# w_down's long passes: four pairs a half in seven products, in the order of gate and up, and loads queued as buffers come free

## The chip, the cores and the metric

The kernel runs on one core of one Trainium2 chip. The metric is the device time of one launch in microseconds (us). Before the change it is 1049.4 us, the median of three runs (1048.66 to 1050.55).

## The reference, cut to what matters

One transformer layer over 256 tokens of width 2048, all in fp32. The first part (input projection, attention, convolution, output projection) is left as it is by the change. The second part is a SwiGLU feed-forward with hidden width 5632:

```python
hn = rms_norm(h, norm2_g)
a  = einsum('bsd,df->bsf', hn, w_gate)          # 2048 x 5632
bu = einsum('bsd,df->bsf', hn, w_up)            # 2048 x 5632
h  = h + einsum('bsf,fd->bsd', silu(a) * bu, w_down)   # 5632 x 2048
```

## The kernel before

**Splitting.** TensorE multiplies in a rounded format, so every fp32 operand is split into a rounded part `hi` and a residue `lo = x - hi`, and a product takes three matmuls: hi·hi, lo·hi, hi·lo. Weights come in by DMA on SP's queue. ScalarE (ACT) rounds them to `whi` (L320). VectorE (DVE) makes the residue `wlo` (L329). For some weights a DMA on GpSimd's (POOL's) queue makes it instead: ACT writes the negated rounding (L323) and the DMA accumulates the raw weight onto it (L324).

**Units.** Gate, up and down work in *units* on 128x512 weight tiles. A *two* is two row tiles of one weight (`g` the first column block, `u` the second), 12 matmuls, one load of 512 KB, one `whi`, one `wlo`. A *pair* (`s`) takes two row tiles of both column blocks at once and multiplies them by a Strassen scheme in seven products instead of eight: 21 matmuls for what two twos do in 24. It costs more beside TensorE: two loads of 512 KB into `wb`, three sums on DVE (`wt`, L966 to L968), two roundings on ACT (`wh`, L969 and L972), two residues on DVE (`wlb` L975, `wlt` L976). All seven products of a pair write PSUM banks `q`, and when the last pair of a block is done `bank_sums` (L1092 to L1099) combines the banks on ACT and DVE.

**Blocks and groups.** The hidden width is worked in 11 blocks of 512, in groups of 4, 4 and 3. After the blocks of a group, `down_pass` multiplies their activations by the rows of w_down that belong to them, in two *halves* of 1024 output columns each. A gate/up block (from the second on) has four pairs and eight twos in the order `sggsggsuusuu`. A half of a long down pass (a group of four blocks) has two pairs and twelve twos, `gguuggsguugsuu` and `sgggugggusuuuu`. The results are added to `hd` in DRAM by accumulating DMAs on POOL's queue (L1138, L1155).

**Activations.** At the end of a block, `block_done` adds the last banks (L1113), multiplies gate by up (L1115), and `transposed` turns the product on TensorE (`ps_a`, L831) and splits it into `ahi` and `alo` (L840, L842). The operands of the down pairs are seven sums of activations, split as well; `make_down_forms` makes them during the last blocks of a group.

**Order.** Each engine runs its instructions in the order in which the program issues them. `run_chunks` issues unit after unit: loads and roundings up to three units ahead, residues two units ahead. Generators (`start`, `resume`, `lag`) put the work between blocks a given number of half units later. DVE and ACT are therefore queues: a late instruction holds up all that stand behind it.

Of the kernel before, what the change touches and what calls it, by code (L numbers as in the profile page):

```python
# [12 lines left out]
F32 = mybir.dt.float32  # L13
# [5 lines left out]
P = 128  # L19
# [76 lines left out]

HI_AHEAD, LO_AHEAD = 3, 2

PAIR_AHEAD = 6

FIRSTS = [sum(FGROUPS[: g + 1]) for g in range(len(FGROUPS))]

# [20 lines left out]
def tile_block(  # L123
# [262 lines left out]

    def run_chunks():
        n = len(chunks)
        i = j = p = 0
        behind = [k for k in range(n) if chunks[k].get("kind") == "s"][NS]  # L390
        for t in range(n):
            hi_lead, lo_lead = lead(t)
            while j < min(i, t + 1 + lo_lead):
                chunks[j]["split"](chunks[j])
                j += 1
            while p < min(n, t + 1 + PAIR_AHEAD):
                if chunks[p].get("kind") == "s":

                    if p < behind and p > t + hi_lead:
                        break  # L400
                    load_pair(chunks[p])
                p += 1
            while i < min(n, t + 1 + hi_lead):
                if i in before:
                    before[i]()
                chunks[i]["load"](chunks[i])
                chunks[i]["round"](chunks[i])
                i += 1
                if hi_lead == lo_lead:
                    chunks[j]["split"](chunks[j])  # L410
                    j += 1
            while j < min(n, t + 1 + lo_lead):
                chunks[j]["split"](chunks[j])
                j += 1
            chunks[t]["multiply"](chunks[t])
# [403 lines left out]
        yield from transposed(j, aa)  # L819

    def transposed(j, aa):
        last = j + 1 in FIRSTS
        b = j - group_of(j)[1]
        for t in range(N // P // 2):

            pool_, tag = (acc_ps, "acc") if last else (aux_ps, "aux")
            pt = pool_.tile([P, 2, S], F32, tag=tag, name="ps_a")
            for i in range(2):
                for m in range(NM):
                    c = (2 * t + i) * P  # L830
                    pe.transpose(pt[:, i, m * P : (m + 1) * P], aa[m][:, c : c + P], ident)  # L831
            if b < 2 and 2 * t < ND:
                raw_act[b] = lhs.tile([P, 2, S], F32, tag=("lhi", "llo")[b], name=f"ar{j}")
                act.copy(raw_act[b], pt)
                yield from lag(3 if last else 6)
                if b:
                    start(make_down_forms(group_of(j)[0]))
# [19 lines left out]

    def make_down_forms(g):

        fp = ffn["pool"]  # L860
        gap = lambda: lag(5 if FGROUPS[g] == 4 else 2)
        a11, a21 = (raw_act[0][:, :, m * P : (m + 1) * P] for m in range(NM))
        a12, a22 = (raw_act[1][:, :, m * P : (m + 1) * P] for m in range(NM))

        hi = fp.tile([P, 7, ND, P], F32R, tag="dhi", name="dhi")
        lo = fp.tile([P, 3, ND, P], F32R, tag="dlo", name="dlo")
        fa, fb = (lhs.tile([P, 2, ND, P], F32, tag=t, name="dsums") for t in ("lhi", "llo"))
        act.copy(hi[:, 0], a11)
        dve.scalar_tensor_tensor(fa[:, 0], a21, -1.0, a22, ALU.mult, ALU.subtract)
        yield from gap()  # L870
        act.copy(hi[:, 1], a12)
        dve.scalar_tensor_tensor(fa[:, 1], fa[:, 0], -1.0, a11, ALU.mult, ALU.subtract)
        yield from gap()
        act.activation(hi[:, 2], a22, AF.Copy, scale=-1.0)
        dve.tensor_tensor(fb[:, 0], a11, a21, ALU.subtract)
        yield from gap()
        act.copy(hi[:, 3:5], fa)
        dve.tensor_tensor(fb[:, 1], a12, fa[:, 1], ALU.subtract)
        yield from gap()
        act.copy(hi[:, 5:7], fb)  # L880
        for i, a in ((0, a11), (1, a12)):
            dve.tensor_tensor(lo[:, i], a, hi[:, i].bitcast(F32), ALU.subtract)
            yield from gap()
        dve.scalar_tensor_tensor(lo[:, 2], a22, -1.0, hi[:, 2].bitcast(F32), ALU.mult, ALU.subtract)
        yield from gap()
        pairs = [lhs.tile([P, 2, ND, P], F32R, tag=t, name="dlo2") for t in ("lhi", "llo")]
        for i, f in ((0, fa), (1, fb)):
            dve.tensor_tensor(pairs[i], f, hi[:, 3 + 2 * i : 5 + 2 * i].bitcast(F32), ALU.subtract)
            yield from gap()
        los = [lo[:, 0], lo[:, 1], lo[:, 2], pairs[0][:, 0], pairs[0][:, 1], pairs[1][:, 0], pairs[1][:, 1]]  # L890
        down_forms[g] = {f: (hi[:, i], los[i]) for i, f in enumerate((0, 1, 3, 4, 5, 6, 2))}

    forms = {}
# [144 lines left out]
    def fast_block(order, pairs, twos, sources, operands, half, whole, by_dma=dict(g=(), u=())):  # L1040

        units, sums = [], {}
        left = dict(s=list(pairs), g=list(twos), u=list(twos))
        for kind in order:
            what = left[kind].pop(0)
            c = dict(kind=kind, sums=sums, done=None, first={}, last={}, rows=what["rows"], **operands)
            if kind == "s":
                c.update(p=what["p"], load=lambda c: None, round=round_pair, split=split_pair, multiply=multiply_pair,
                         uses=[q for q, _, _ in PRODUCTS])
# [12 lines left out]
        units[-1].update(done=whole, prompt=True)  # L1062
        chunks.extend(units)
# [8 lines left out]

    def down_pass(g, j0, nb):
        k0 = j0 * HD
        ks = [k for k in range(nb * HD) if k >= 2 * HD or k % HD >= ND]
        twos = [dict(ks=(k0 + a, k0 + b), rows=slice(k0 + a, k0 + b + 1, b - a), k=None)
                for a, b in zip(ks[::2], ks[1::2])]
        for i, order in enumerate(DORDERS[nb]):
            n = 2 * i
            end = {}  # L1080
            fast_block(order, [dict(p=p, rows=slice(k0 + p, k0 + p + HD + 1, HD)) for p in range(ND)], twos,
                       dict(g=(w_down, n * N), u=(w_down, (n + 1) * N)),
                       dict(pairs=lambda: down_forms.get(g), plain=actT.get),
                       lambda sums, n=n, end=end: down_half(g, n, sums, end),
                       lambda sums, n=n, end=end: down_whole(g, n, sums, end))

    halfway = {}

# [19 lines left out]
    def block_done(j, q):  # L1108
# [4 lines left out]
            dve.tensor_tensor(u[m], q[i], u[m], ALU.add)  # L1113
# [18 lines left out]

    def down_half(g, n, q, end):
        gs, us = yield from bank_sums(q)
        for m in range(NM):
            cs = slice(n * N, (n + 1) * N)
            if not at_end(g, n):
# [10 lines left out]
    def down_whole(g, n, q, end):  # L1148
# [3 lines left out]
        for m, i in enumerate((Q3, QX)):  # L1152
            if not at_end(g, n):
                dve.tensor_tensor(us[m], q[i], us[m], ALU.add)
                pool.dma_start(out=hd[m][:, (n + 1) * N : (n + 2) * N], in_=us[m], accum_op=ALU.add)  # L1155
                continue
            w = N // 2
            for a in range(0, N, w):
                hs = hend[m][:, N + a : N + a + w]
                dve.tensor_tensor(hs, hs, q[i][:, a : a + w], ALU.add)  # L1160
                sp.dma_start(out=out[m * P : (m + 1) * P, (n + 1) * N + a : (n + 1) * N + a + w], in_=hs)
        if g == len(FGROUPS) - 1 and not at_end(g, n):
            fetch_end()

# [82 lines left out]
```

## Time and profile before

| | |
|---|---|
| median of 3 runs | 1049.4 us |
| profiled execution | 1048.92 us, span 1047.1 us |
| PE busy | 1036.2 us, 99% |
| DVE busy | 900.6 us, 86% |
| ACT busy | 621.6 us, 59% |
| granted TensorE clock | 1.00 |

The page gives busy time for each engine, and the chain of waits that ended last. A matmul's row shows how long it is in flight, about 390 ns, and matmuls overlap: what one costs is the distance from its start to the next one's. The timeline view lists instructions of an engine in order of time with start and duration; in square brackets stands idle time before it and what ended that.

### The profile page before, as it was taken

The numbers are of one execution on the slowest core, as the hardware profiler recorded it, in microseconds if no ns is written. First come the engines' busy times: TensorE is split into PE (matmuls) and PEld (weight loads), VectorE is DVE, ScalarE is ACT, GpSimd is POOL, SyncE is SP. The second block draws the span as 40 slices with busy tenths as digits, with TensorE's granted clock in tenths as the row PEclk, the third lists the DMA queues.
The fourth block names the chain that finished last, engine by engine and source line by source line (L and its number), as shares of the span: only waits on it lengthen the run. The fifth ranks groups of instructions, "written<-read, shape, count | busy, mean of one in ns | idle before, by whom it ended". The sixth has DMA issues, their size and how long they took to land.

```text
span 1047.1 us, 12933 instructions
## 1 busy us (share of the span) xinstructions
PE 1036.2 (99%) x4663; PEld 852.5 (81%) x4663; DVE 900.6 (86%) x1095; ACT 621.6 (59%) x786; POOL 100.5 (10%) x143
## 2 busy tenths in 40 slices
PE   9999999999999999999999999999999999999998
PEld 7888887877788788888888888888888888888886
DVE  7899889898765599999787898999878789989897
ACT  7544666755756565776463657666644446657442
POOL 0130122201100100000001010000000110000010
PEclk9999999999999999999999999999999999999999
DMA  9657654453546566987867789879757879798683
GB/s 335 227 182 280 212 163 167 154 181 134 177 153 226 194 223 214 268 266 236 232 210 188 217 271 273 256 217 285 248 175 241 219 208 291 222 287 267 187 265 85
DMA packets 113936, 231.30 MB, mean 221 GB/s; under 512 B 7504, under 2 KB 8656, under 8 KB 113616
## 3 DMA queue, kind: packets, MB, share of 16 engines
q1 hardware_dynamic: 104864, 203.71, 56.9%
q0 software_dynamic: 8864, 26.74, 13.4%
q8 instruction: 36, 0.59, 0.2%
q14 instruction: 28, 0.23, 0.1%
q10 hardware_dynamic: 144, 0.03, 0.0%
HBM read 204.24 MB, written 9.44 MB: 204 GB/s over the span
## 4 chain that ended last, share of the span: by engine, by line
PE 61%; DMA 2%; DVE 2%; issue 1%; ACT 0%; DVEq 0%; POOLq 0%
PE q L1020 12%; PE q L1014 12%; PE q L1015 12%; PE q L995 8%; PE q L993 7%; PE q L994 7%; DMA raw<-in_w_down_dram 1%; PE ps_a L831 1%; DMA wlo<-raw 1%; PE acc L365 1%; PE acc L359 1%; PE acc L360 1%; DVE wlo L329 1%; DVE wlt L976 0%; DVE wt L966 0%
## 5 line engine op out<-in xcount | busy, mean ns | idle before, releaser
L320 ACT CAST whi<-raw 128x1024 fp32r<-128x1024 f32 (+1 forms) x273 | 281.5, 1048 | 141.6 <-PE acc L360 58.9
L329 DVE TENSOR_TENSOR wlo<-raw,whi 128x1024 fp32r<-128x1024 f32 (+1 forms) x239 | 287.8, 1218 | 73.5 <-ACT whi L320 73.3
L972 ACT CAST wh<-wt 128x2048 fp32r<-128x2048 f32 x52 | 99.6, 1914 | 77.6 <-DVE wt L968 76.9
L976 DVE TENSOR_TENSOR wlt<-wt,wh 128x2048 fp32r<-128x2048 f32 x52 | 119.1, 2290 | 14.9 <-ACT wh L972 14.7
L359 PE MATMUL acc<-whi,xhi 128*128 128x512 f32 x320 | 126.9, 397 | 1.0 <-ACT whi L320 0.9
L360 PE MATMUL acc<-whi,xlo 128*128 128x512 f32 x320 | 125.2, 391 | 0.0
L1014 PE MATMUL q<-whi,chi 128*128 128x512 f32 x320 | 125.2, 391 | 0.0
L1015 PE MATMUL q<-whi,clo 128*128 128x512 f32 x320 | 124.5, 389 | 0.0
L993 PE MATMUL q<-wh,fhi 128*128 128x512 f32 x280 | 109.9, 393 | 0.0
L994 PE MATMUL q<-wh,flo 128*128 128x512 f32 x280 | 109.1, 390 | 0.0
L517 DVE SCALAR_TENSOR_TENSOR y<-upad,cw,y 128x256 f32<-128x256 f32 x240 | 102.2, 482 | 2.2 <-ACT y L510 2.2
L1014 PE MATMUL q<-whi,ahi 128*128 128x512 f32 x256 | 100.2, 391 | 0.0
L1015 PE MATMUL q<-whi,alo 128*128 128x512 f32 x256 | 99.6, 389 | 0.0
L975 DVE TENSOR_TENSOR wlb<-wb,wh 128x1536 fp32r<-128x1536 f32 x52 | 91.1, 1752 | 1.8 <-ACT wh L969 1.8
L365 PE MATMUL acc<-wlo,xhi 128*128 128x512 f32 x320 | 87.8, 396 | 2.0 <-DVE wlo L329 2.0
L1020 PE MATMUL q<-wlo,chi 128*128 128x512 f32 x320 | 85.7, 390 | 0.2 <-DMA wlo<-raw 0.2
L969 ACT CAST wh<-wb 128x1536 fp32r<-128x1536 f32 x52 | 76.6, 1474 | 0.0
L365 PEld LDWEIGHTS acc<-wlo,xhi 128*128 128x128 f32 x320 | 59.7, 189 | 15.3 <-DVE wlo L329 3.3
L359 PEld LDWEIGHTS acc<-whi,xhi 128*128 128x128 f32 x320 | 60.4, 189 | 14.3 <-ACT whi L320 1.9
L1020 PEld LDWEIGHTS q<-wlo,chi 128*128 128x128 f32 x320 | 59.9, 188 | 13.2 <-DMA wlo<-raw 0.8
L360 PEld LDWEIGHTS acc<-whi,xlo 128*128 128x128 f32 x320 | 60.4, 189 | 12.2
L1014 PEld LDWEIGHTS q<-whi,chi 128*128 128x128 f32 x320 | 60.1, 188 | 12.3
(230 smaller groups left out, 1739.1 us busy)
## 6 DMA issues: line engine op xcount, KB each, us to landing
raw<-in_w_in_dram SPq DMA_DIRECT2D x79, 512.0 KB, 4.6
raw<-in_w_down_dram SPq DMA_DIRECT2D x64, 512.0 KB, 7.2
raw<-in_w_gate_dram SPq DMA_DIRECT2D x48, 512.0 KB, 7.5
raw<-in_w_up_dram SPq DMA_DIRECT2D x48, 512.0 KB, 6.2
wb<-in_w_up_dram SPq DMA_DIRECT2D x40, 512.0 KB, 3.7
wb<-in_w_gate_dram SPq DMA_DIRECT2D x40, 512.0 KB, 4.9
wlo<-raw POOLq DMA_DIRECT2D x34, 512.0 KB, 7.1
raw<-in_w_out_dram SPq DMA_DIRECT2D x32, 512.0 KB, 4.2
```

The costliest lines, as they stand in the source:

```text
L320: act.copy(c["hi"], c["raw"])
L329: dve.tensor_tensor(c["lo"], c["raw"], c["hi"].bitcast(F32), ALU.subtract)
L359: pe.matmul(ps[m], xhi[:, ms], hi[:, j, :], start=c["first"] and j == 0, stop=False)
L360: pe.matmul(ps[m], xlo[:, ms], hi[:, j, :], start=False, stop=False)
L365: pe.matmul(ps[m], xhi[:, ms], lo[:, j, :], start=False, stop=c["last"] and j == nk - 1)
L517: dve.scalar_tensor_tensor(y[:, ct, :], src, wk, y[:, ct, :], ALU.mult, ALU.add)
L976: dve.tensor_tensor(lot, c["t"], c["hi"][:, :SUMMED].bitcast(F32), ALU.subtract)
L993: pe.matmul(ps, hi, c["hi"][:, w], start=bool(first), stop=False)
L994: pe.matmul(ps, lo, c["hi"][:, w], start=False, stop=False)
L1014: pe.matmul(ps, xs[i][0][:, ms], hi[:, i, :], start=i == 0 and bool(c["first"].get(qs[m])), stop=False)
L1015: pe.matmul(ps, xs[i][1][:, ms], hi[:, i, :], start=False, stop=False)
L1020: pe.matmul(sum_bank(c, qs[m]), xs[i][0][:, ms], lo[:, i, :], start=False, stop=i == 1 and bool(c["last"].get(qs[m])))
```

## The change

It does four things.

- The long passes (`NDS = (4, 4, 2)`, two before) take four pairs and eight twos a half, in the order of gate and up, `sggsggsuusuu`. The short pass keeps its orders.
- The residues of three twos a half (the third `g`, the second and fourth `u`) come by DMA on POOL's queue; before, a down pass had none.
- The forms of the down pairs grow with it: operands of 128x512 instead of 128x256, eleven instructions on DVE. All activations of a group's first two blocks are kept raw.
- Weight loads of all later blocks are issued in the order in which their buffers come free (`load_freed`). Lags around the ends of blocks and the accumulating DMAs move (`HD_LAG`, `closing`).

```diff
-ND = 2
-DORDERS = {4: ("gguuggsguugsuu", "sgggugggusuuuu"), 3: ("gguusggsuu", "gggsgsuuuu")}
+NDS = (4, 4, 2)
+DORDERS = {4: (ORDER, ORDER), 3: ("gguusggsuu", "gggsgsuuuu")}
+HD_LAG = 3
+DOWN_BY_DMA = {4: (dict(g=(2,), u=(1, 3)),) * 2, 3: (dict(g=(), u=()),) * 2}
...
+        def freed(side, t):
+            if not ahead[side]:
+                return None
+            k = (raws, pairs)[side][place[side][ahead[side][0]] - (RAW_BUFS, PAIR_BUFS)[side]]
+            return k if k in split and (t >= k or not chunks[k]["by_dma"]) else None
+
+        def load_freed(t):
+            while True:
+                ready = [(k, side) for side in range(2) if (k := freed(side, t)) is not None]
+                if not ready:
+                    return
+                load(ahead[min(ready)[1]].pop(0))
...
-            yield from lag(1 if last else 4)
+            yield from lag(1 if last else 3 if closing(j) else 4)
+
+    def closing(j):
+        return j + 1 in FIRSTS and NDS[group_of(j)[0]] == HD
...
+        one = lambda tag, dt, name: lhs.tile([P, 4, P], dt, tag=tag, name=name)[:, :nd]
...
+        f4, f5, f6, f2 = (one(t, F32, "dsums") for t in ("lhi", "lhi", "llo", "llo"))
...
+        dve.tensor_tensor(lo[3], f2, hi[3].bitcast(F32), ALU.subtract)
+        yield from gap()
+        ls = ffn["pool"].tile([P, 4, nd, P], F32R, tag="draw", name="dls")
+        act.copy(ls[:, 3], f6)
+        for i, (f, h) in enumerate(((f4, hs[:, 0]), (f5, hs[:, 1]), (f6, ls[:, 3]))):
+            dve.tensor_tensor(ls[:, i], f, h.bitcast(F32), ALU.subtract)
...
-        yield from lag(4)
+        yield from lag(6 if closing(j) else 4)
         yield from transposed(j, u)
...
+        if not at_end(g, n):
+            if FGROUPS[g] > 3:
+                yield from lag(HD_LAG)
+            for m in range(NM):
+                pool.dma_start(out=hd[m][:, (n + 1) * N : (n + 2) * N], in_=us[m], accum_op=ALU.add)
```

On DVE, where the last gate/up block of a long group ends and its down pass begins (before: `sum` is what `bank_sums` and `block_done` write, `wlo` the residue of a two, `wt` a sum of a pair):

```order
L1094 TENSOR_TENSOR sum_4695<-q_4424,sum_4694 128x512
L1095 TENSOR_TENSOR sum_4696<-q_4428,sum_4695 128x512
L1096 TENSOR_TENSOR sum_4697<-q_4432,sum_4696 128x512
L1097 TENSOR_TENSOR sum_4695<-q_4432,sum_4695 128x512
L1098 TENSOR_TENSOR sum_4694<-q_4444,sum_4694 128x512
L1099 TENSOR_TENSOR sum_4696<-q_4436,sum_4696 128x512
L329 TENSOR_TENSOR wlo<-raw,whi 128x1024
L1113 TENSOR_TENSOR sum_4695<-q_4449,sum_4695 128x512
L1113 TENSOR_TENSOR sum_4697<-q_4627,sum_4697 128x512
L1115 TENSOR_TENSOR sum_4695<-sum_4695,sum_4694 128x512
L1115 TENSOR_TENSOR sum_4697<-sum_4697,sum_4696 128x512
L329 TENSOR_TENSOR wlo<-raw,whi 128x1024 x3
```

The same place after the change, from the last residue before it on (`dls` are residues of the down pairs' forms, on line 933; the sums are now L1140 to L1145, L1159 and L1161, the pair's sums L1011 to L1013, its residues L1020 and L1021):

```order
L331 TENSOR_TENSOR wlo<-raw,whi 128x1024
L933 TENSOR_TENSOR dls<-dsums,dhs 128x512 x2
L1011 TENSOR_TENSOR wt<-wb 128x1024
L1012 TENSOR_TENSOR wt<-wb,wt 128x512
L1013 TENSOR_TENSOR wt<-wt,wb 128x512
L1020 TENSOR_TENSOR wlb<-wb,wh 128x1536
L1021 TENSOR_TENSOR wlt<-wt,wh 128x2048
L933 TENSOR_TENSOR dls<-dsums,dls 128x512
L1140 TENSOR_TENSOR sum_4724<-q_4431,sum_4723 128x512
L1141 TENSOR_TENSOR sum_4725<-q_4435,sum_4724 128x512
```

```order
L331 TENSOR_TENSOR wlo<-raw,whi 128x1024
L1159 TENSOR_TENSOR sum_4724<-q_4455,sum_4724 128x512
L1159 TENSOR_TENSOR sum_4726<-q_4639,sum_4726 128x512
L1161 TENSOR_TENSOR sum_4724<-sum_4724,sum_4723 128x512
L1161 TENSOR_TENSOR sum_4726<-sum_4726,sum_4725 128x512
L331 TENSOR_TENSOR wlo<-raw,whi 128x1024
L1011 TENSOR_TENSOR wt<-wb 128x1024
L1012 TENSOR_TENSOR wt<-wb,wt 128x512
L1013 TENSOR_TENSOR wt<-wt,wb 128x512
L1020 TENSOR_TENSOR wlb<-wb,wh 128x1536
L1021 TENSOR_TENSOR wlt<-wt,wh 128x2048
```

A whole pair (the down pass's first) and three `dls` now stand ahead of the sums, and a second pair follows the closing sums with one `wlo` between, where twelve twos' residues stood first.

On POOL's queue in the second long down pass, before (`wlo` the residues by DMA, `hd` the accumulating DMAs):

```order
L324 DMA wlo<-raw 128x1024 x14
L1138 DMA hd_85<-sum_6995 128x512
L1138 DMA hd_86<-sum_6997 128x512
L1155 DMA hd_85<-sum_6996 128x512
L1155 DMA hd_86<-sum_6998 128x512
L1138 DMA hd_85<-sum_7261 128x512
L1138 DMA hd_86<-sum_7263 128x512
L1155 DMA hd_85<-sum_7262 128x512
L1155 DMA hd_86<-sum_7264 128x512
L324 DMA wlo<-raw 128x1024 x10
```

And after:

```order
L326 DMA wlo<-raw 128x1024 x17
L1187 DMA hd_85<-sum_7020 128x512
L1187 DMA hd_86<-sum_7022 128x512
L1214 DMA hd_85<-sum_7021 128x512
L1214 DMA hd_86<-sum_7023 128x512
L326 DMA wlo<-raw 128x1024 x3
L1187 DMA hd_85<-sum_7332 128x512
L1187 DMA hd_86<-sum_7334 128x512
L1214 DMA hd_85<-sum_7333 128x512
L1214 DMA hd_86<-sum_7335 128x512
L326 DMA wlo<-raw 128x1024 x10
```

Three residues stand ahead of each half's four accumulations, so those of the second half are queued right behind the four of the first.

More of the change, by code (lines that the diff above doesn't have):

```diff
@@ L388, in run_chunks, with load, split_next @@
         n = len(chunks)
-        i = j = p = 0
-        behind = [k for k in range(n) if chunks[k].get("kind") == "s"][NS]
+        i = j = 0
+        pairs = [k for k in range(n) if chunks[k].get("kind") == "s"]
+        raws = [k for k in range(n) if chunks[k].get("kind") != "s" and not chunks[k].get("spare_raw")]
+        behind = pairs[NS]
+        loaded, split = set(), set()
+        def load(k):
+            if k not in loaded:
+                loaded.add(k)
+                if k in before:
+                    before[k]()
+                chunks[k]["load" if chunks[k].get("kind") != "s" else "fetch"](chunks[k])
+        def split_next():
+            chunks[j]["split"](chunks[j])
+            split.add(j)
+        ahead = [[which[a] for a in range(len(which)) if which[a] >= behind] for which in (raws, pairs)]
+        place = [{k: a for a, k in enumerate(which)} for which in (raws, pairs)]
+        def freed(side, t):
[9 more added lines that the diff above has]
+                load(ahead[min(ready)[1]].pop(0))
         for t in range(n):
@@ L393, in run_chunks @@
             while j < min(i, t + 1 + lo_lead):
-                chunks[j]["split"](chunks[j])
+                split_next()
                 j += 1
[L396 to L402, printed above, removed]
+            if t + hi_lead >= behind - NS:
+                load_freed(t)
             while i < min(n, t + 1 + hi_lead):
-                if i in before:
-                    before[i]()
-                chunks[i]["load"](chunks[i])
+                load(i)
+                for which in ahead:
+                    if i in which:
+                        which.remove(i)
                 chunks[i]["round"](chunks[i])
@@ L821, in transposed @@
     def transposed(j, aa):
-        last = j + 1 in FIRSTS
+        last = j + 1 in FIRSTS and NDS[group_of(j)[0]] < HD
         b = j - group_of(j)[1]
@@ L831, in transposed @@
                     pe.transpose(pt[:, i, m * P : (m + 1) * P], aa[m][:, c : c + P], ident)
[L832 to L834 removed]
+            g = group_of(j)[0]
+            nd = NDS[g]
+            if b < 2 and 2 * t < nd:
+                if not b and not t:
+                    raw_act[g] = ffn["pool"].tile([P, 2, nd, S], F32, tag="draw", name="raw_act")
+                act.copy(raw_act[g][:, b, 2 * t : 2 * t + 2, :], pt)
                 yield from lag(3 if last else 6)
[L836 to L837 removed]
+                if b and 2 * t + 2 == nd:
+                    start(make_down_forms(g))
                 continue
@@ L858, in make_down_forms @@
     def make_down_forms(g):
-        fp = ffn["pool"]
+        nd = NDS[g]
         gap = lambda: lag(5 if FGROUPS[g] == 4 else 2)
[L862 to L867, printed above, removed]
@@ L868, in make_down_forms @@
-        act.copy(hi[:, 0], a11)
-        dve.scalar_tensor_tensor(fa[:, 0], a21, -1.0, a22, ALU.mult, ALU.subtract)
+        raw = raw_act.pop(g)
+        a11, a21 = (raw[:, 0, :, m * P : (m + 1) * P] for m in range(NM))
+        a12, a22 = (raw[:, 1, :, m * P : (m + 1) * P] for m in range(NM))
+        one = lambda tag, dt, name: lhs.tile([P, 4, P], dt, tag=tag, name=name)[:, :nd]
+        hi = [one("lhi", F32R, "dhi") for _ in range(4)]
+        lo = [one("llo", F32R, "dlo") for _ in range(4)]
@@ L885, in make_down_forms @@
         yield from gap()
[L886 to L891, printed above, removed]
+        dve.tensor_tensor(lo[3], f2, hi[3].bitcast(F32), ALU.subtract)
@@ new lines, in make_down_forms @@
+        yield from gap()
[3 more added lines that the diff above has]
+            dve.tensor_tensor(ls[:, i], f, h.bitcast(F32), ALU.subtract)
+            if i:
+                yield from gap()
+        down_forms[g] = {f: (hi[i], lo[i]) for i, f in enumerate((0, 1, 3, 2))}
+        down_forms[g].update({4: (hs[:, 0], ls[:, 0]), 5: (hs[:, 1], ls[:, 1]), 6: (ls[:, 3], ls[:, 2])})
@@ L1047, in fast_block @@
             if kind == "s":
-                c.update(p=what["p"], load=lambda c: None, round=round_pair, split=split_pair, multiply=multiply_pair,
+                c.update(p=what["p"], fetch=load_pair, by_dma=False, round=round_pair, split=split_pair, multiply=multiply_pair,
                          uses=[q for q, _, _ in PRODUCTS])
@@ L1074, in down_pass @@
         k0 = j0 * HD
-        ks = [k for k in range(nb * HD) if k >= 2 * HD or k % HD >= ND]
-        twos = [dict(ks=(k0 + a, k0 + b), rows=slice(k0 + a, k0 + b + 1, b - a), k=None)
-                for a, b in zip(ks[::2], ks[1::2])]
+        nd = NDS[g]
+        ks = [k for k in range(nb * HD) if k >= 2 * HD or k % HD >= nd]
+        twos = [dict(ks=(k0 + a, k0 + b), rows=slice(k0 + a, k0 + b + 1, b - a), k=i)
+                for i, (a, b) in enumerate(zip(ks[::2], ks[1::2]))]
         for i, order in enumerate(DORDERS[nb]):
@@ L1080, in down_pass @@
             end = {}
-            fast_block(order, [dict(p=p, rows=slice(k0 + p, k0 + p + HD + 1, HD)) for p in range(ND)], twos,
+            fast_block(order, [dict(p=p, rows=slice(k0 + p, k0 + p + HD + 1, HD)) for p in range(nd)], twos,
                        dict(g=(w_down, n * N), u=(w_down, (n + 1) * N)),
@@ L1084, in down_pass @@
                        lambda sums, n=n, end=end: down_half(g, n, sums, end),
-                       lambda sums, n=n, end=end: down_whole(g, n, sums, end))
+                       lambda sums, n=n, end=end: down_whole(g, n, sums, end), DOWN_BY_DMA[nb][i])
     halfway = {}
```

34 lines of the change are left out of this document (21 added, 13 removed).

## Prediction

> **What bounds the kernel now.** First the page: span, busy times, the chain's shares by engine. Then busy time by stage, the waits of TensorE, and the timelines of TensorE, VectorE and ScalarE around the end of a group.
>
> ```profile
> span 1047.1 us, 12933 instructions
> ...
> PE 1036.2 (99%) x4663; PEld 852.5 (81%) x4663; DVE 900.6 (86%) x1095; ACT 621.6 (59%) x786; POOL 100.5 (10%) x143
> ...
> PE 61%; DMA 2%; DVE 2%; issue 1%; ACT 0%; DVEq 0%; POOLq 0%
> ```
>
> TensorE is busy 99% of the span, and most of the chain is its own. By stage (us, then busy time of PE, PEld, DVE, ACT, POOL, the granted clock, DMA share, GB/s): three gate/up blocks of the first group, then the two long down passes.
>
> ```profile
> 391.00:517.10 126.10, 125.80 (x565) 103.50 (x564) 114.28 (x113) 81.07 (x79) 8.67 (x10) 1.00 0.81 243
> 517.10:602.50 85.40, 85.40 (x381) 70.52 (x380) 70.93 (x68) 43.26 (x39) 5.25 (x6) 1.00 0.70 205
> 768.70:854.10 85.40, 85.40 (x381) 70.51 (x381) 70.90 (x68) 43.20 (x39) 5.24 (x6) 1.00 0.69 205
> ```
>
> The two passes take 85.4 us each, at full clock. DVE fills 114.3 of 126.1 us (91%) where the order is that of gate and up, and 70.9 of 85.4 (83%) in a pass. So the change goes the right way: fewer matmuls where TensorE is full, paid for by an engine with room. The question is whether DVE has the room at each place.
>
> TensorE's timeline gives the price of a matmul and the dates to meet. First a block's start, its second pair and that pair's first matmul on `wlt`; then two twos in a row; then the start of the first long pass, and its first pair.
>
> ```profile
> 475.36 0.39 PE L993 MATMUL q<-wh,fhi 128*128 128x512 f32 x1
> ...
> 486.02 0.39 PE L993 MATMUL q<-wh,fhi 128*128 128x512 f32 x1
> ...
> 486.47 0.39 PE L995 MATMUL q<-wlt,fhi 128*128 128x512 f32 x1
> ...
> 501.47 0.39 PE L1014 MATMUL q<-whi,chi 128*128 128x512 f32 x1
> ...
> 504.19 0.39 PE L1014 MATMUL q<-whi,chi 128*128 128x512 f32 x1
> ...
> 517.11 0.39 PE L1014 MATMUL q<-whi,ahi 128*128 128x512 f32 x1
> ...
> 534.84 0.49 PE L995 MATMUL q<-wlt,dhi 128*128 128x512 f32 x1
> 535.17 0.40 PE L993 MATMUL q<-wh,dhi 128*128 128x512 f32 x1
> ```
>
> Twelve matmuls take 504.19 - 501.47 = 2.72 us: 0.227 us each. A block's second pair needs its `wlt` 486.47 - 475.36 = 11.11 us after the block's start.
>
> VectorE's timeline in the last block of the first group (476 to 517 us), and one pair of the block before with nothing between its parts (454.77 to 461.63):
>
> ```profile
> 454.77 1.22 DVE L966 TENSOR_TENSOR wt<-wb 128x1024 f32<-128x1024 f32 x1
> ...
> 459.42 2.29 DVE L976 TENSOR_TENSOR wlt<-wt,wh 128x2048 fp32r<-128x2048 f32 x1 [0.31 <-ACT wh L972]
> 461.63 0.42 DVE L875 TENSOR_TENSOR dsums<-ar 128x256 f32<-128x256 f32 x1
> ...
> 475.11 1.29 DVE L1113 TENSOR_TENSOR sum<-q,sum 128x512 f32<-128x512 f32 x2 [0.56 <-PE q L1020]
> ...
> 477.51 1.22 DVE L966 TENSOR_TENSOR wt<-wb 128x1024 f32<-128x1024 f32 x1
> ...
> 483.19 2.29 DVE L976 TENSOR_TENSOR wlt<-wt,wh 128x2048 fp32r<-128x2048 f32 x1 [1.00 <-ACT wh L972]
> ...
> 486.00 1.22 DVE L329 TENSOR_TENSOR wlo<-raw,whi 128x1024 fp32r<-128x1024 f32 x1
> 487.13 0.42 DVE L884 SCALAR_TENSOR_TENSOR dlo<-ar,dhi 128x256 fp32r<-128x256 f32 x1
> 487.46 1.22 DVE L329 TENSOR_TENSOR wlo<-raw,whi 128x1024 fp32r<-128x1024 f32 x1
> ...
> 495.65 0.69 DVE L888 TENSOR_TENSOR dlo<-dsums,dhi 128x512 fp32r<-128x512 f32 x1
> 496.26 1.22 DVE L329 TENSOR_TENSOR wlo<-raw,whi 128x1024 fp32r<-128x1024 f32 x1
> ...
> 502.25 2.29 DVE L976 TENSOR_TENSOR wlt<-wt,wh 128x2048 fp32r<-128x2048 f32 x1
> 504.45 1.22 DVE L329 TENSOR_TENSOR wlo<-raw,whi 128x1024 fp32r<-128x1024 f32 x1
> ...
> 511.13 0.69 DVE L1094 TENSOR_TENSOR sum<-q,sum 128x512 f32<-128x512 f32 x1 [2.57 <-ACT sum L1092]
> ...
> 514.53 0.68 DVE L1099 TENSOR_TENSOR sum<-q,sum 128x512 f32<-128x512 f32 x1
> ```
>
> The tight place is the second pair of every block: `wlt` is done at 483.19 + 2.29 = 485.48 and needed at 486.47, so 0.99 us is left. That chain cannot start sooner: DVE waits for TensorE at the block's end (475.11), closes the block, and only then reaches the pair (477.51).
>
> **The change part by part.**
>
> *Matmuls.* Two more pairs a half take 42 matmuls and replace four twos with 48: 6 fewer a half, 24 in the two long passes (the program has 4356 of this size before, 4332 after). 24 x 0.227 = **5.44 us less**, all on TensorE, hence on the path. That they go is certain; only their price is not.
>
> The Trainium skill ("TensorE: Matmul & The Clock Gate", Back-to-back issue gap) gives about 131 ns for a matmul of 512 columns in a sustained stream; the row says 227 ns, and by the page the gain would be an estimated 3.1 us.
>
> *The old passes' own wait.* The first pair's first `wlt` matmul takes 535.17 - 534.84 = 0.33 us instead of 0.23, having waited for DVE. The new first pair is made well ahead: **0.1 us less** in each pass, 0.2 together.
>
> *DVE's share.* In a half, two pairs (6.86 us each, 454.77 to 461.63) take the place of four twos' residues, and three further residues leave for DMA: seven at 1.13 us (486.00 to 487.13). That adds 13.7 - 7.9 = 5.8 us to a half of about 35.5, some 41.3 against 40.9 us of matmuls (180 x 0.227) if the waits inside a pair counted in full; they overlap other work, and a block of the same order lives with as much. Within a half it is hidden, except where a chain has a date.
>
> *The date that is missed.* At the end of the last block DVE's queue now holds the whole first pair, and the forms are larger. Walked in the clock of the profiled execution:
>
> 1. Up to the third `wlt` of that block (504.45 when it lets the next one in): four form residues at 0.61 us (495.65 to 496.26) stand where two at 0.33 (487.13 to 487.46) and two at 0.61 stood, 0.55 more, of which 0.27 falls into the idle 1.00 ahead of 483.19. DVE is at 504.73.
> 2. A `wlo` (1.13), two `dls` (1.22), a pair (6.86) and a `dls` (0.61): 514.55. Before, DVE had idled 2.57 us here and begun the sums at 511.13. It is now 3.4 us late.
> 3. The six sums take 514.53 - 511.13 + 0.60 = 4.0 us, a `wlo` 1.13, the closing four 477.51 - 475.11 = 2.40, a `wlo` 1.13: the pass's second pair starts at 523.21.
> 4. Its `wlt` is ready 459.42 + 2.29 - 454.77 = 6.94 us later: 530.15.
> 5. TensorE wants it at 517.11 + 11.11 = 528.22.
>
> TensorE waits **1.9 us**, once in each long pass: 3.9 us. After that it is behind DVE again: the next pair has 10.2 us of matmuls (45 x 0.227) against some 8.6 us on DVE (a pair, a `wlo` and one 0.6 us residue of activations). At the turn from one half to the next the closing multiply is absent (half of the 2.40), which makes up for the extra `wlo`, so about the 0.99 us is left there. Bounds: if DVE were on time at the block's end, the same chain gives 475.11 to 477.51, one `wlo` and 6.94: 10.2 us after the start, no wait, so 0; if a pair lost another 1.0 us to ACT in each of steps 2 and 4, the wait is 3.9. I take the walk, near the middle.
>
> *Residues by DMA.* The three that move cost TensorE nothing if they land in time.
>
> ```profile
> raw<-in_w_down_dram SPq DMA_DIRECT2D x64, 512.0 KB, 7.2
> ...
> hd<-sum POOLq DMA_DIRECT2D x20, 256.0 KB, 6.8
> ...
> DMA to landing us min/median/max: 5.0/7.1/10.2
> ```
>
> The last row is that of L324: 5.0 to 10.2 us. The third `g` of a half follows the late pair. ACT can only round it after that pair's `wh`: DVE's three sums end some 2.6 us after 523.21, `wh` is done by 527.8, a rounding and a negation of about 1 us each end at 529.7, and POOL issues near 530.1. TensorE uses it after the rest of the pair (19 matmuls), four transposes (0.46) and 8 matmuls: 530.2 + 6.6 = 536.8. That leaves 6.7 us; in the second half, with no wait but four accumulations of 256 KB just ahead on the queue, some 7.6. The median fits the second and misses the first by 0.4; the shortest fits both; the longest is late by 3.5 and 2.6. I take 0: at that moment one pair's two loads are in flight, less than the mean DMA share of 0.81 in the gate/up stage, where the slow ones arise. The upper end stays in the range.
>
> The Trainium skill ("DMA: Bandwidth & Descriptors", Anatomy of one DMA) fits a POOL DMA at 2.0 us plus its bytes over 436 GB/s, an estimated 3.2 us for 512 KB; no row is below 5.0, so the rows decide; by the page the DMAs would never be late.
>
> *Loads as buffers come free, other lags.* Loads start earlier; among TensorE's waits no load stands, so nothing is gained, and a burst beside a residue can cost. 0, and up to 2 us either way. The short pass keeps its order, and its forms their size: 0.
>
> **The sum.** 1048.92 - 5.44 - 0.2 + 3.9 = 1047.2 us for the profiled execution, 1.8 less. It lies 0.5 below the median of the runs, so **1047.6 us** against 1049.4. About 0.2% (2.1 us) is what a measurement of this kernel can tell from no change: the forecast is just inside it.
>
> **The rivals.**
>
> *DVE is less late* (faster). For it: at 511.13 it idled 2.57 us, and slack is made up within a block. If the wait is at most 1.2 us a pass, the gain is 5.64 - 2.4 = 3.2 us: 1046.2; with no wait 1043.8. Against: every step above is a row, and the queue is in order. 20%.
>
> *The third `g`'s residue lands late* (slower). Queued behind four accumulations and beside a pair's loads, it takes 8.4 us: late by 1.7 in the first half and 0.8 in the second, 5.0 over both passes: 1047.6 + 5.0 = 1052.6. At 10.2 us it would be 1059.8. It decides from 3.9 us of lateness in all, at about 8.1 us each. For it: a median of 7.1 against 6.7 us. Against: DVE's lateness also holds up loads, which leaves the DMA engines freer. 22%.
>
> *Residues in gate/up blocks slip*, as loads come in another order: a handful of waits under 1 us, some 2.5 us together: 1050.1. 10%.
>
> **How the numbers follow.** Forecast 48%. Its own uncertainty (0.4 us a pass) puts a quarter of it, 12%, beyond 2.1 us. Faster: 12 + 20 = 32%. Same: 36 and 6 of the last rival's 10: 42%. Slower: 22 + 4 = 26%. The range goes from near the middle of the first rival, 1045.0, to the price of the second, 1052.8; beyond lie a DVE that is on time and DMAs of 10 us.
>
> **What would show it.** 24 matmuls fewer, and long passes of about 84.5 us (85.4 - 2.7 - 0.1 + 1.9). Among TensorE's waits a `wlt` wait of about 1.9 us in each pass, some 11 us after its start; sums of the last block beginning at about 514.5 instead of 511.1. The forecast is wrong if that wait is absent or twice as long, if TensorE waits for `wlo` by DMA by more than 1 us a pass, or if stages other than the two passes change.

## The result and the profile after

The changed kernel takes 1058.74 us (median of five, 1058.34 to 1060.41), the kernel before 1049.17 us beside it: a ratio of 1.0092, interval 1.0077 to 1.0107. It is slower by 0.9%, outside the range of 1045.0 to 1052.8 us. The page after: span, busy times, and the chain's shares by engine.

```profile
span 1057.0 us, 12990 instructions
PE 1036.7 (98%) x4639; PEld 851.1 (81%) x4639; DVE 924.8 (87%) x1109; ACT 646.1 (61%) x804; POOL 110.8 (10%) x155
PE 55%; DVE 5%; issue 3%; DMA 2%; ACT 1%; SPq 0%; DVEq 0%; POOL 0%; POOLq 0%; ACTq 0%
```

The 24 matmuls are gone (4639 against 4663), yet PE is busy as long as before: where fewer instructions take the same busy time, some ran slower. Busy time by stage, with the columns of the prediction's table: the gate/up blocks of the first group, then the two long passes.

```profile
391.30:526.60 135.30, 129.47 (x566) 105.63 (x566) 119.79 (x114) 83.41 (x79) 8.67 (x10) 0.97 0.79 235
526.60:611.50 84.90, 83.31 (x369) 68.12 (x368) 78.86 (x75) 53.62 (x46) 10.46 (x12) 1.00 0.88 253
777.60:864.10 86.50, 84.91 (x370) 69.31 (x369) 79.17 (x75) 53.49 (x46) 10.44 (x12) 0.98 0.86 249
```

The passes are near the forecast (84.9 and 86.5 us, forecast 84.5). The loss is in a stage that the forecast left alone: 126.1 us of gate/up blocks have become 135.3, which the prediction had named as a sign of being wrong. TensorE's waits over the whole run, the longest first, say for what:

```profile
PE q L1040 <- DVE wlt L1021: 3.4, 3, 1.6
PE q L1065 <- DMA wlo<-raw: 3.2, 2, 2.4
PE q L1059 <- ACT whi L322: 2.6, 1, 2.6
```

The first is the forecast wait in the passes (1.6 us each by this list, and a small one that was there before). The others lie at the end of the second gate/up block, the first with pairs (its order is `gsggsgsuusuu`, `FIRST_ORDER` in the kernel, and not that of the later blocks), and one of 0.8 us early in the third. TensorE's timeline there, then at the second pair of each long pass:

```profile
433.48 0.80 PE L1059 MATMUL q<-whi,chi 128*128 128x512 f32 x1 [2.60 <-ACT whi L322]
434.07 0.63 PE L1060 MATMUL q<-whi,clo 128*128 128x512 f32 x1
434.50 0.63 PE L1059 MATMUL q<-whi,chi 128*128 128x512 f32 x1
...
439.38 1.66 PE L1065 MATMUL q<-wlo,chi 128*128 128x512 f32 x4 [2.42 <-DMA wlo<-raw]
...
452.70 1.20 PE L1065 MATMUL q<-wlo,chi 128*128 128x512 f32 x4 [0.78 <-DMA wlo<-raw]
...
537.69 0.40 PE L1039 MATMUL q<-wh,dls 128*128 128x512 f32 x1
539.68 0.50 PE L1040 MATMUL q<-wlt,dhs 128*128 128x512 f32 x1 [1.59 <-DVE wlt L1021]
...
788.68 0.40 PE L1039 MATMUL q<-wh,dls 128*128 128x512 f32 x1
790.67 0.50 PE L1040 MATMUL q<-wlt,dhs 128*128 128x512 f32 x1 [1.59 <-DVE wlt L1021]
...
791.47 0.62 PE L1040 MATMUL q<-wlt,dls 128*128 128x512 f32 x1
791.88 0.63 PE L1038 MATMUL q<-wh,dhs 128*128 128x512 f32 x1
```

Two things cost here: the waits, and after some of them matmuls that start 0.43 us apart instead of 0.227 (434.07 to 434.50). Adding up, from all PE rows from 380 us on, what each start-to-start distance over 0.3 us has beyond 0.227:

| excess, us | before | changed | difference |
|---|---|---|---|
| second block and start of the third (400 to 460) | 0.79 | 9.83 | +9.04 |
| first long pass | 0.29 | 2.50 | +2.21 |
| second long pass | 0.28 | 3.91 | +3.63 |
| all else | 2.60 | 2.67 | +0.07 |

That is +14.95; less the 5.44 of the matmuls, +9.5, and the span grew by 9.9 (0.4 of it before this stretch). So 9 us of the loss lies around one block's end. What it waited for is on SP's queue. SP's issues before:

```profile
410.15 0.37 SPq L956 DMA_DIRECT2D wb<-in_w_up_dram  x1
410.56 0.47 SPq L956 DMA_DIRECT2D wb<-in_w_gate_dram  x1
411.07 0.98 SPq L315 DMA_DIRECT2D raw<-in_w_up_dram  x2
```

and after:

```profile
410.53 0.37 SPq L1001 DMA_DIRECT2D wb<-in_w_up_dram  x1
410.94 0.47 SPq L1001 DMA_DIRECT2D wb<-in_w_gate_dram  x1
419.90 0.37 SPq L1001 DMA_DIRECT2D wb<-in_w_up_dram  x1
420.31 0.47 SPq L1001 DMA_DIRECT2D wb<-in_w_gate_dram  x1
420.82 0.47 SPq L317 DMA_DIRECT2D raw<-in_w_up_dram  x1
421.33 1.29 SPq L317 DMA_DIRECT2D raw<-in_w_gate_dram  x2
428.85 0.37 SPq L317 DMA_DIRECT2D raw<-in_w_up_dram  x1
```

The block's last two `up` loads were issued together at 411 us. Now loads of the third block stand ahead of them. The first of the two is held behind that block's second pair, which waits for its buffer until 419.90 us, and goes out 9.8 us later than before. The second reaches the head of the queue behind two `gate` loads, at 422.6 us, and then waits for a buffer of its own. SP's waits from 395 to 445 us have the two parts of it:

```profile
SPq L317 <- DMA raw<-in_w_up_dram: 3.8, 1, 3.8
SPq L317 <- DVE wlo L331: 2.4, 1, 2.4
```

The twos share five load buffers (`RAW_BUFS = 5`), and four hold `gate` tiles of the third block that went ahead; the first of these is rounded at 437.45 us. So the last `up` has to take the buffer of the `up` before it, must wait until that has landed and its residue is made, and goes out 17.3 us later than before. It is the one that TensorE waits for, first for its rounding (433.48), then for its residue (439.38). ScalarE, which rounds the two, shows the same:

```profile
426.51 1.05 ACT L322 CAST whi<-raw 128x1024 fp32r<-128x1024 f32 x1 [6.36 <-DMA raw<-in_w_up_dram]
432.38 1.05 ACT L322 CAST whi<-raw 128x1024 fp32r<-128x1024 f32 x1 [4.82 <-DMA raw<-in_w_up_dram]
```

The way in is `if t + hi_lead >= behind - NS: load_freed(t)`: it lets loads of the third block go when the second block still has four units to load.

### The profile page after: what moved, and what is told of

Same layout as the page of the kernel before. It is cut to its first block, busy times and chain, and to the rows that moved or that the text cites. A ratio compares the mean times of both kernels' runs of the same rounds, so it can differ in the third digit from the quotient of the medians.

```text
span 1057.0 us, 12990 instructions
## 1 busy us (share of the span) xinstructions
PE 1036.7 (98%) x4639; PEld 851.1 (81%) x4639; DVE 924.8 (87%) x1109; ACT 646.1 (61%) x804; POOL 110.8 (10%) x155
## 4 chain that ended last, share of the span: by engine, by line
PE 55%; DVE 5%; issue 3%; DMA 2%; ACT 1%; SPq 0%; DVEq 0%; POOL 0%; POOLq 0%; ACTq 0%
PE q L1065 10%; PE q L1059 9%; PE q L1060 9%; PE q L1040 8%; PE q L1038 8%; PE q L1039 8%; DVE wlo L331 1%; DVE wt L1011 1%; DMA raw<-in_w_up_dram 1%; PE acc L367 1%; ACT wh L1017 1%; PE ps_a L863 1%; DVE wlt L1021 1%; PE acc L362 1%; PE acc L361 1%
## 5 line engine op out<-in xcount | busy, mean ns | idle before, releaser
L322 ACT CAST whi<-raw 128x1024 fp32r<-128x1024 f32 (+1 forms) x257 | 266.1, 1050 | 118.3 <-PE acc L362 58.9
L331 DVE TENSOR_TENSOR wlo<-raw,whi 128x1024 fp32r<-128x1024 f32 (+1 forms) x211 | 254.8, 1218 | 50.3 <-ACT whi L322 50.0
L1017 ACT CAST wh<-wt 128x2048 fp32r<-128x2048 f32 x60 | 114.9, 1915 | 96.8 <-DVE wt L1013 96.8
L1021 DVE TENSOR_TENSOR wlt<-wt,wh 128x2048 fp32r<-128x2048 f32 x60 | 137.4, 2291 | 17.0 <-ACT wh L1017 16.6
L1020 DVE TENSOR_TENSOR wlb<-wb,wh 128x1536 fp32r<-128x1536 f32 x60 | 105.1, 1752 | 10.6 <-ACT wh L1014 10.6
L326 POOL DMA_DIRECT2D wlo<-raw x46 | 39.8, 866 | 527.6 <-ACT wlo L325 360.4
L1014 ACT CAST wh<-wb 128x1536 fp32r<-128x1536 f32 x60 | 88.5, 1476 | 1.9 <-DMA wb<-in_w_gate_dram 1.9
L1059 PE MATMUL q<-whi,ahi 128*128 128x512 f32 x192 | 74.9, 390 | 0.0
L1060 PE MATMUL q<-whi,alo 128*128 128x512 f32 x192 | 74.7, 389 | 0.0
L1011 DVE TENSOR_TENSOR wt<-wb 128x1024 f32<-128x1024 f32 x60 | 73.1, 1219 | 1.3 <-DMA wb<-in_w_gate_dram 1.3
```

The costliest lines, as they stand in the source:

```text
L322: act.copy(c["hi"], c["raw"])
L331: dve.tensor_tensor(c["lo"], c["raw"], c["hi"].bitcast(F32), ALU.subtract)
L1017: act.copy(c["hi"][:, :SUMMED], c["t"])
L1020: dve.tensor_tensor(lob, c["b"][:, 1:], c["hi"][:, SUMMED:].bitcast(F32), ALU.subtract)
L1021: dve.tensor_tensor(lot, c["t"], c["hi"][:, :SUMMED].bitcast(F32), ALU.subtract)
L1059: pe.matmul(ps, xs[i][0][:, ms], hi[:, i, :], start=i == 0 and bool(c["first"].get(qs[m])), stop=False)
```

## Experiments

All ratios are to the kernel before, run beside each, with a 95% interval.

**The old load order, all else as changed.**

```diff
-            if t + hi_lead >= behind - NS:
-                load_freed(t)
+            while p < min(n, t + 1 + PAIR_AHEAD):
...
+                    chunks[p]["fetch"](chunks[p])
```

> The changed kernel with the loads issued in the old order, all else (four pairs a half, DMA residues, lags) as changed. Theory A (the loss is the handover to the new load order in the second block: 9.4 us of waits and lowered clock around 430 to 453 us): that stretch is as before, long passes keep their wlt wait of about 1.8 us, time 1058.7 - 9.4 = about 1049.3 us. Rival B (the four-pair halves, their forms and DMA residues cost the time, whatever the loads): about 1058 us.

Measured: 1072.49 us, 1.0234 (1.0219 to 1.0250). Neither theory. The second block is as before (its excess is 0.6 us), so theory A holds for that place; but the long passes now have 14.2 and 14.3 us of excess. TensorE's timeline at the third `g`'s residue of the first pass:

```profile
537.67 0.39 PE L1031 MATMUL q<-whi,alo 128*128 128x512 f32 x1
542.35 1.97 PE L1036 MATMUL q<-wlo,ahi 128*128 128x512 f32 x4 [4.29 <-DMA wlo<-raw]
```

SP's issues ahead of it:

```profile
528.52 0.88 SPq L972 DMA_DIRECT2D wb<-in_w_down_dram  x2
529.50 0.93 SPq L317 DMA_DIRECT2D raw<-in_w_down_dram  x2
```

and POOL's issue of that residue:

```profile
531.02 0.89 POOL L326 DMA_DIRECT2D wlo<-raw  x1 [20.87 <-ACT wlo L325]
```

The residue's DMA starts right behind four loads of 512 KB issued within 2 us, and lands at 542.30, 11.3 us later; these waits come four times, 3.1 to 4.6 us each. That is the prediction's rival "the third `g`'s residue lands late", and it shows under the old order, not in the changed kernel. The new order is not an ornament of the change: the residues by DMA need it.

**The new order, handed over cleanly.** The third block's loads go only when the second block's are all issued (its first pair may go as before).

```diff
-            if not ahead[side]:
+            if not ahead[side] or any(k < behind and k not in loaded for k in (pairs if ahead[side][0] == behind else raws)):
                 return None
```

> The changed kernel, but loads are issued as buffers come free only once the second block's own loads have all been issued (its first later pair alone may go ahead, as before). Theory A: no whi wait in the second block, about 1049.3 us. If loads as buffers come free hurt in later blocks as well, or theory B holds: 1052 to 1058 us.

Measured: 1048.71 us, 1.0006 (0.9997 to 1.0016), as theory A has it: 10 us back. The second block's excess is 1.3 us. The same residue has two loads close ahead of it instead of four:

```profile
528.19 0.88 SPq L1001 DMA_DIRECT2D wb<-in_w_down_dram  x2
533.05 4.15 SPq L317 DMA_DIRECT2D raw<-in_w_down_dram  x2
```

It is issued at 530.69 and lands at 536.81, after 6.1 us, in time. The DMA engines are full meanwhile in both kernels (share 1.00 in these 6.1 us, 0.96 in the 11.3 us under the old order), so a residue shares them with what was issued ahead of it; that this alone makes the difference is read from the two traces and not tested by a run.

**The new load order alone, on the kernel before.** `run_chunks` of the changed kernel in the kernel before, two pairs a half.

```diff
-                    load_pair(chunks[p])
+            if t + hi_lead >= behind - NS:
+                load_freed(t)
```

> The kernel before, with the new load order alone (two pairs a half, no DMA residues in the long passes, old lags). Theory A: the same waits in the second block, 1049.2 + 9 = about 1058 us, passes as before. Rival B: 1049 to 1050 us.

Measured: 1058.29 us, 1.0100 (1.0085 to 1.0115). The whole loss without a single new pair; the block's excess is 10.4 us, the passes are as before. Rival B is out.

**One waiting pair left in the queue.** As the clean handover, but the third block's second pair still goes ahead of the two `up` loads.

```diff
-for k in (pairs if ahead[side][0] == behind else raws)
+for k in (raws, pairs)[side]
```

> The changed kernel, with only one thing left of the early handover: no two's load of a later block goes ahead of the second block's own, but one pair's two loads (the third block's second pair) still stand ahead of that block's last two up loads on SP's queue. They wait for their buffer's last reader, wlb, done at 426.2 us. If the loss is own loads queued behind a load that waits: the two up loads are issued at about 427 us instead of 411, land near 434, and TensorE, which wants the first at 430.5, waits some 5 us, with the lowered clock behind it 5 to 8 us: 1054 to 1057 us. If the loss came from buffers taken by early loads of twos, or from crowded DMA: about 1048.7 us as with the clean handover.

Measured: 1054.78 us, 1.0061 (1.0043 to 1.0080); the five runs lie from 1051.35 to 1057.08. So one pair that waits in the queue, with no two's buffer taken, costs some 6 of the 10 us in the median. That this lies in the expected range is in part luck, since a date was misread: the pair waits for the `wlb` that ends at about 418 us, not 426. SP in the profiled run:

```profile
417.85 0.37 SPq L1001 DMA_DIRECT2D wb<-in_w_up_dram  x1
418.26 0.47 SPq L1001 DMA_DIRECT2D wb<-in_w_gate_dram  x1
418.77 0.98 SPq L317 DMA_DIRECT2D raw<-in_w_up_dram  x2
```

The `up` loads are 7.6 us late there, and TensorE waits 1.6, 0.7 and 1.8 us. This run is the fastest of the five, at a mean granted clock of 1.000; the slowest, 1057.08, has 0.995. Against the 1048.7 us of the clean handover the five runs lie 3 to 8 us higher, the slower ones at a lower clock. The last `up` goes out right behind the one before it here; the 6.2 us that it waits for a buffer in the changed kernel are missing, and no run has them alone.

**The clean order alone, with two pairs a half.** The gate of the second experiment added to the third.

> The kernel before, with two pairs a half, and the new load order with the clean handover. The price of the order by itself. If it only serves the four-pair halves, which are late by DMA without it (1072.5 against 1048.7 us): 1048 to 1050 us, no change. If loads as buffers come free gain by themselves: below 1047; if they crowd residues by DMA, 1050 or more.

Measured: 1049.39 us, 1.0011 (1.0002 to 1.0020). By itself the order gains nothing.

**Without residues by DMA, clean and old order.**

```diff
-DOWN_BY_DMA = {4: (dict(g=(2,), u=(1, 3)),) * 2,
+DOWN_BY_DMA = {4: (dict(g=(), u=()),) * 2,
```

> The same kernel without residues by DMA in the long passes: DVE has three more (3 x 1.13 = 3.4 us) in each half, 44.7 against 40.9 us of matmuls. If DVE's share of a half binds, TensorE waits some 2 to 4 us in each of four halves: 1055 to 1062 us. If DVE has slack enough within a half: 1049 to 1051.

> The changed kernel with the old load order (1072.5 us) and without residues by DMA in the long passes. If there the old order hurts only through late residues by DMA (four waits of 3.4 to 4.8 us and the lowered clock behind them, some 24 us): about as the kernel without them and with the new order, within 3 us of it. If the pairs' own loads come late too: clearly slower than that one.

Measured: 1052.34 us, 1.0042 (1.0026 to 1.0059), and 1053.30 us, 1.0048 (1.0033 to 1.0063). The first lies between the two ranges expected, nearer to that of slack; the second is within 3 us of it, as expected. Without the DMA residues TensorE waits 1.1 us more for `wlt` in the second half of each pass and 0.7 in the block behind it, 3.6 in all, where DVE was given 4 x 3.4 = 13.6 us: it has slack for most of that. And once no residue goes by DMA, the load order is worth 1 us, within the noise, instead of 24: it matters to the pairs through the residues.

**The forms earlier; a `g` ahead of the pair.** Two ways to take DVE's queue off the date at a pass's start, both on the clean handover.

```diff
-        gap = lambda: lag(5 if FGROUPS[g] == 4 else 2)
+        gap = lambda: lag(4 if FGROUPS[g] == 4 else 2)
```

```diff
-DORDERS = {4: (ORDER, ORDER),
+DORDERS = {4: (FIRST_ORDER, ORDER),
```

> As the kernel whose handover waits for the second block's loads (1048.7 us), with the steps of the down pairs' forms 4 half units apart instead of 5: their last three residues (3 x 0.6 us) leave the stretch of DVE's queue ahead of a pass's second pair. If the wlt wait (1.76 us a pass) is that queue: it is gone or below 0.3 us, about 1045.2 us. If the wait comes from ACT or from loads: no change, 1048.7.

> The same kernel with a g two moved ahead of the first pair in the first half of a long pass (gsggsgsuusuu): DVE's chain up to the second pair is as long as before, TensorE needs it one two (12 x 0.227 = 2.7 us) later. If the wait is a date missed by 1.8 us: gone, about 1045.2 us, unless the third pair (now one two behind the second, 7.5 us of matmuls against 6.9 us and a residue on DVE) is late by about 0.5 to 1 us: 1046 to 1047. If DVE is short of time over the whole half rather than at one date: no gain.

Measured: 1051.49 us, 1.0029 (1.0017 to 1.0041), and 1055.36 us, 1.0066 (1.0051 to 1.0081). Both expectations failed. TensorE's waits in the first pass, with the forms earlier:

```profile
PE q L1060 <- DVE alo L877: 1.8, 1, 1.8
PE q L1040 <- DVE wlt L1021: 0.9, 1, 0.9
```

The `wlt` wait shrank from 1.6 to 0.9 us, but `alo`, the last block's activations, became the next late thing: DVE makes it at 538.74 behind the next pair's residues, with the clean handover alone at 535.53 ahead of them. With the `g` first the same wait is longer still (2.4 us). Shifting the order moved another instruction behind a pair.

**First two `g` by DMA, and first and third.** DVE's queue made shorter without moving anything on it.

```diff
-DOWN_BY_DMA = {4: (dict(g=(2,), u=(1, 3)),) * 2,
+DOWN_BY_DMA = {4: (dict(g=(0, 1), u=(1, 3)), dict(g=(2,), u=(1, 3))),
```

> As the kernel whose handover waits for the second block's loads, and in the first half of a long pass the residues of the first two g come by DMA instead of that of the third: DVE has two residues of 1.13 us less ahead of the pass's second pair. If the wlt wait there is DVE's queue as walked (2.26 us less against 1.8 us of wait), both waits and the lowered clock behind the second one go, 1.76 x 2 + 1.35 = 4.9 us: about 1044.5 us. If the wait is ACT's or a load's: 1048 to 1050 us. If residues by DMA in the last block come late: slower than that.

> As the variant with the residues of the first two g of a pass by DMA (1046.3 us), but the first and the third instead. DVE has 1.13 us less ahead of the second pair: the wlt wait falls from 1.76 to about 0.6 us a pass, and the waits for the second g's residue (0.3 and 1.04 us) go: 1046.5 us, the same within 1 us. If ACT or POOL were what makes residues late at the pass's start, the first g is late now: 1048 or more.

Measured: 1046.34 us, 0.9982 (0.9973 to 0.9992), and 1046.89 us, 0.9987 (0.9978 to 0.9997): both faster than the kernel before. In the first variant both `wlt` waits are gone, so they were DVE's queue; but the second `g`'s residue is late by 0.3 and 1.04 us. In the second variant that residue is made on DVE again, and the `wlt` wait is 0.8 us a pass, near the 0.6 expected. ScalarE's timeline in the first variant shows why:

```profile
513.82 0.56 ACT L1138 COPY sum<-q 128x512 f32<-128x512 f32 x1
518.35 1.23 ACT L1151 ACTIVATE sum<-sum 128x512 f32<-128x512 f32 x2 [3.97 <-DVE sum L1144]
519.48 1.04 ACT L322 CAST whi<-raw 128x1024 fp32r<-128x1024 f32 x1
520.42 1.05 ACT L325 ACTIVATE wlo<-raw 128x1024 fp32r<-128x1024 f32 x1
```

ACT stands idle for DVE's late sums with the silu at its head and the second `g`'s rounding behind it.

**The silu behind that rounding.**

```diff
     def products_done(j, q):
         g, u = yield from bank_sums(q)
+        if closing(j):
+            yield from lag(1)
         for t in g:
             act.activation(t, t, AF.Silu)
```

> As the variant with the residues of the first two g of a long pass by DMA (1046.3 us), with the last block's silu issued one half unit later. There ACT stood idle 3.97 us at 514.4 us for DVE's sums, with the second g's rounding queued behind the silu, so that its DMA was issued at 521.83 and TensorE waited 0.3 and 1.04 us for it. Now that rounding stands ahead of the silu and falls into the idle time. If ACT's order is what makes that residue late: issued some 5 us earlier, both waits go, 1046.3 - 1.3 = about 1045.0 us. If the DMA engines are what is short there: the residue lands no earlier, 1046.3 us. If the silu comes late for block_done: slower.

Measured: 1044.77 us, 0.9965 (0.9952 to 0.9979), and both waits are gone. The rounding now runs in the idle time, the DMA is issued at 516.76 instead of 521.83:

```profile
514.40 1.05 ACT L322 CAST whi<-raw 128x1024 fp32r<-128x1024 f32 x1
515.35 1.06 ACT L325 ACTIVATE wlo<-raw 128x1024 fp32r<-128x1024 f32 x1
518.48 1.23 ACT L1153 ACTIVATE sum<-sum 128x512 f32<-128x512 f32 x2 [2.07 <-DVE sum L1144]
```

The passes of this kernel, with next to nothing left to wait for in the first and 0.5 us for a residue by DMA in the second:

```profile
517.60:600.50 82.90, 82.81 (x370) 68.23 (x369) 77.43 (x74) 51.54 (x44) 9.56 (x12) 1.00 0.93 268
766.50:850.00 83.50, 82.96 (x370) 68.32 (x370) 77.55 (x74) 51.53 (x44) 9.67 (x12) 1.00 0.92 266
```

85.4 - 82.9 = 2.5 us in the first pass: nearly the 2.7 that twelve matmuls are worth. This version is faster than both kernels, by 0.35% than the one before.

## Why the prediction was wrong, point by point

- **Matmuls, -5.44 us.** Right: 24 fewer, and the last experiment's passes are shorter by 2.5 and 1.9 us at 0.227 us a matmul.
- **The date that is missed, +3.9 us.** Right, step by step. The pass starts 9.48 us later in the changed kernel (526.59 against 517.11). Taking that off, the sums begin at 524.02 - 9.48 = 514.54 (walk: 514.55), and `wlt` lets TensorE go on at 539.68 - 9.48 = 530.20 (walk: 530.15). The wait is 1.76 us (539.68 - 537.69 - 0.23; walk: 1.9), twice. What the walk lacked is the lowered clock behind a wait: none in the first pass, in the second seven steps of 0.43 us, some 1.4 us.
- **The old passes' own wait, -0.2 us.** It doesn't show: new small steps took the place of the old ones.
- **Residues by DMA, 0.** Right for the changed kernel: the third `g`'s residue was issued at 539.55 and landed 6.1 us later, in time. The reason given, "one pair's two loads are in flight", is true only under the new load order; under the old one there were four, and it took 11.3 us.
- **Loads as buffers come free, "0, and up to 2 us either way".** This is the step that failed: it measured 9.0 us, of which some 6 are waits beyond the old ones and some 3 slowed matmuls. The step asked whether TensorE waited for a load before; it did not ask which loads now stand ahead of which on SP's queue, whether they can go when they reach its head, and whose buffers they take. The clean handover gives the loss back (1048.71 us) and the new order alone has it (1058.29 us). The queue's order alone would have shown `gate` and `wb` of the third block ahead of `up` of the second, and SP's waits before, from 395 to 445 us, have the warning:

```profile
SPq L956 <- DVE wlb L975: 47.9, 6, 11.9
```

  SP's queue stood still 47.9 us in six waits there; TensorE waited for none of it, as what stood behind was wanted later. The rival "residues in gate/up blocks slip" named the stage and the reordered loads, but as waits under 1 us for residues, 2.5 us in all.
- **The sum.** With 9.0 in the place of 0, and 1.9 for what the passes lost beyond the forecast wait (2.21 + 3.63 - 3.9; 1.4 of it slowed matmuls), 1047.2 becomes 1058.1 us; the profiled execution took 1058.74. With the handover mended the change can't be told from none (1.0006, interval 0.9997 to 1.0016), as the forecast said of it, though it lies above the forecast's own number, 1047.6 against 1049.4 us or 0.9983.

## What to carry to other kernels

Where loads are issued in the order in which buffers come free, check the place where the old order hands over to the new: no load that must wait may stand ahead of one that the running stage still needs, since the queue is served in order, and none may take the last buffer that one needs. When an order looks like a side effect of a change, take it out alone: here it was the whole loss, at its handover, and also what the DMA residues of the gain need (24 us without it). And when a wait is taken away by moving work on a full engine, look for the next date on that engine; giving the work to another engine, without moving the rest, was what paid.

## What was not expected of the hardware

After a wait of TensorE the granted clock can fall to half: matmuls then start 0.43 us apart for some 3.4 us, some 1.3 to 1.6 us of loss. The length of the wait alone doesn't decide it. Of the two 1.76 us waits of the changed kernel one was followed by slow matmuls and one was not; with the old load order a wait of 3.1 us (803.13 us) had none behind it, one of 4.1 us (584.66) seven. By windows, the granted clock from 430 to 445 us is 0.77 in the changed kernel, 0.66 with the new load order alone.

What the traces show beside it is how a wait lies in time. In all fourteen the granted clock changes only at dates a whole number of steps of 3.41 us apart. Cut at these dates, the stretches around the changed kernel's two 1.76 us waits are (columns as in the table by stage, the granted clock third from the end):

```profile
535.47:538.88 3.41, 2.62 (x11) 1.58 (x9) 3.10 (x2) 3.41 (x3) 0.00 (x0) 1.00 0.17 38
538.88:542.29 3.41, 2.61 (x12) 2.15 (x13) 3.07 (x4) 3.13 (x4) 0.89 (x1) 1.00 1.03 332
788.06:791.47 3.41, 1.82 (x8) 0.97 (x7) 2.98 (x2) 3.41 (x5) 0.86 (x1) 1.00 0.60 171
791.47:794.88 3.41, 3.41 (x11) 2.65 (x10) 3.16 (x4) 1.52 (x2) 0.00 (x0) 0.50 1.08 281
```

The first wait is split over two stretches, 0.79 and 0.80 us idle; the second falls whole into one, 1.59 us, and the next stretch has half the clock. Over all traces, from 20 us on, each of the eight stretches at full clock with 1.96 us or more of idle TensorE was followed by one at half, one of the nine from 1.53 to 1.82 us was, and none with less. The 3.1 us wait is split into 1.80 and 1.17; of the 4.1 us wait 1.82 and 2.07 fall into two stretches, and the clock drops behind the second, at 590.28 us. That the idle time within such a stretch decides is read from these traces; no run tests it alone.

The Trainium skill ("TensorE: Matmul & The Clock Gate", HAM oscillation) puts the fall at idle gaps of more than about 3.4 us; these rows show it after 1.76 us. The same page (section "Wait — 56ns, not 53.3ns?") gives 426.7 ns between matmuls of 512 columns at the low clock, and the rows agree: 434.07 to 434.50. So a wait of 2 us is to be priced with some 1.5 us behind it, sometimes.
